# Where the split halves of the expert table lie, and when two small transposes are queued, in the second half of a streaming encoder layer

## The chip, the cores and the metric

The kernel runs on one core of a Trainium2 chip. A core has five engines with instruction queues of their own: PE (TensorE, matrix multiplies), DVE (VectorE), ACT (ScalarE), POOL (GpSimd) and SP (SyncE, which here only starts transfers). Each engine works through its queue in order, and semaphores tie the queues together. The metric is the device time of one launch in microseconds (us), the median of several runs.

## The reference, cut to what matters

One layer of an encoder for 384 tokens: 128 tokens of eight short sequences (the "sample" tokens) and 256 tokens of one prompt. After a recurrent branch and a sparse-attention branch comes PEER, a mixture of 16384 tiny experts, and only that part is touched here:

```python
q = (hb @ w_pq).reshape(PEER_BLOCK, PEER_HEADS, 2, PEER_DHALF)
s = jnp.einsum('nhpd,hpkd->nhpk', q, peer_keys).astype(jnp.float32)
s1, i1 = lax.top_k(s[:, :, 0], PEER_TOPK)
s2, i2 = lax.top_k(s[:, :, 1], PEER_TOPK)
...
sc, j = lax.top_k(cand, PEER_TOPK)
e = jnp.take_along_axis(cidx, j, axis=-1)
g = jax.nn.softmax(sc, axis=-1)
act = jax.nn.gelu(jnp.einsum('nhkd,nd->nhk', peer_u[e], hb).astype(jnp.float32))
return jnp.einsum('nhk,nhkd->nd', (g * act).astype(hb.dtype), peer_v[e])
```

Each token takes 8 x 16 = 128 of the 16384 experts. Expert e has a row of 1024 numbers in `peer_u` and one in `peer_v`.

## The kernel before

**Two ways through the experts.** For the 128 sample tokens the kernel gathers: 128 indirect transfers on POOL's queue (L1568, "picks"), each of 128 rows of 2048 numbers, into a ring of three buffers `raw`; DVE takes a product with a running sum (L1575), ACT the gelu (L1576, L1577), DVE adds the weighted row to `acc` (L1581). For the 256 prompt tokens it computes all 16384 experts densely, in 128 tiles of 128 experts: `dense_u(j)` loads tile j of the transposed `peer_u` (512 KB, into one of four buffers `w`) and multiplies it with the tokens `h2f`; gelu (L1484) puts the result in `G`. Later `weights` builds the matrix of picked weights out of one-hot products and multiplies it into G, and `dense_v` multiplies with `peer_v`.

**Two kinds of u tile.** Tiles 0 to 35 (N1 = 36) are multiplied as plain fp32, 8 matmuls of the program that appear as 16 in the profile. Tiles 36 and up are split first: ACT writes the high part `wh` (L230), DVE the low part `wl` (L234), and PE does 24 faster matmuls with the split tokens `h2h`, `h2l`. The split parts lie in a pool of their own, `halves2`, four buffers for wh and three for wl, 4 KB per partition each (28 KB).

**Selection.** `peer_select(i)` finds the 128 picks of each token of token tile i (i = 0: sample; 1 and 2: prompt): scores on PE, then some hundred small DVE instructions. For i = 1 and 2 it ends in three PE transposes of the result (indices `idx`, named pix in the profile, and weights `gw`, named pg; L1379) and one ACT copy into `pT` (L1381), which `weights` reads much later.

**Memory.** A partition's memory is handed out as two stacks, one growing from each end. At the left stand const, stream (the w buffers), and from L1656 on peer (raw, acc, h2h, h2l) and the pool of G. At the right stand hpool2, then qpool (h2f 8 KB, keysT 4 KB, qp 12 KB, ioe 0.5 KB), then sel (the selection's scratch, with idx and gw, about 31 KB). By the addresses that this kernel is given, 6,048 bytes are left between the end of G and the lower end of sel. So halves2 (L1679) is opened after `qs.close()` has closed qpool and sel, at the right end, where both lay. `late` (gA, gO) and the pool `wb` of `weights` follow below it.

**Order.** The program is written in the order of L1647 to L1724, and a scheduler then makes each engine's queue out of it: by a timing model of its own it runs the program and takes, for an engine that is free, the earliest instruction of the text that is ready. So picks, which the text spreads over the u tiles, stand far ahead, between the instructions of the selection. What is fixed at that point stays fixed: on the chip each queue runs in order. In `dense_v`'s loop a pick also waits for the matmuls of the fifth tile before (`pace`).

Of the kernel before, what the change touches and what calls it, by code (L numbers as in the profile page):

```python
# [182 lines left out]
OFF = [j for j in range(NW, 128) if (j - NW + 1) * NB // (128 - NW) > (j - NW) * NB // (128 - NW)]  # L183
AHEAD = sorted(OFF + [j for j in range(NW, 128) if j not in OFF][:NA - 1])
LAST, EARLY = 126, 108
WB, EB = (4, 4, 3), 3
UENG, VENG, GENG, VN = 'v', 'v', 'g', 3
SENG = 'gv'
# [7 lines left out]
class K:  # L196
# [1094 lines left out]
    def peer_select(self, i, h0=0, nh=8):  # L1291

        nc = self.nc
# [4 lines left out]
        for hb in range(0, nh, 4):  # L1298
            for half in range(2):
                pr = slice(64 * half, 64 * half + 64)  # L1300
                p = self.ps([128, 4, 128], tag="dx")
# [44 lines left out]
        idx = self.t([128, 2, 8, 16], tag="pix", bufs=2)[:, :, :nh]  # L1346
# [15 lines left out]
        gw = self.t([128, nh, 16], tag=f"pg{i}{h0}", pool=self.pool if i else self.hpool2)  # L1362
# [6 lines left out]
        gw = gw.rearrange("p a b -> p (a b)")  # L1369
        if i == 0:  # L1370
# [3 lines left out]
            nc.vector.tensor_copy(e, ef.rearrange("p h k -> p (h k)"))  # L1374
            return e, gw

        p = self.ps([128, 3, 128], tag="dx")
        for q, src in enumerate((idx[:, 0].rearrange("p h k -> p (h k)"), idx[:, 1].rearrange("p h k -> p (h k)"), gw)):
            nc.tensor.transpose(p[:, q], src, self.ident)  # L1379
        T = self.t([128, 3, 128], tag=f"pT{i}", pool=self.hpool2)  # L1380
# [85 lines left out]
    def dense_u(self, j):  # L1466

        nc = self.nc
        u = self.expert(self.I["puT"][j].rearrange("p k e -> p (k e)"))
        p = self.ps([128, 256], tag="u")  # L1470
        if j < N1:
            u = u.rearrange("p (k e) -> p k e", k=8)
            for k in range(8):
                self.mm(p, u[:, k], self.h2f[:, k], start=(k == 0), stop=(k == 7))
        else:
            uh, ul = (x.rearrange("p (k e) -> p k e", k=8) for x in self.split(u, UENG[j % len(UENG)]))
            hi, lo = self.h2p
            for k in range(8):
                self.mm(p, uh[:, k], hi[:, k], start=(k == 0), stop=False)
                self.mm(p, uh[:, k], lo[:, k], start=False, stop=False)  # L1480
                self.mm(p, ul[:, k], hi[:, k], start=False, stop=(k == 7))
        off = j in OFF
        g = self.G[:, j] if j < NW else self.t([128, 256], tag="gO" if off else "gA", bufs=2 if off else NA, pool=self.late)
        nc.scalar.activation(g, p, AF.Gelu_apprx_tanh)  # L1484
        if off:
            nc.sync.dma_start(self.Ad[OFF.index(j)], g)
        return g
# [97 lines left out]
    def run(self):  # L1585
        hs = self.ctx.enter_context(ExitStack())
        self.halves = self.open(hs, "halves")
        with ExitStack() as front:
            fh = front.enter_context(ExitStack())
            self.fconst = self.open(fh, "fconst")  # L1590
            self.hpool = self.open(fh, "hpool")
            self.fill = self.open(fh, "fill")
            self.psum = self.open(self.ctx, "psum", space=bass.MemoryType.PSUM)
            self.lo_pattern = "v"
            with ExitStack() as s:
                self.pool = self.open(s, "ph")
                self.setup()
                self.mod_head()
                self.front_x()
                self.front_h()  # L1600

                self.early = {name: self.raw(self.win_ap(name)) for name in ("wa", "wb", "wg")}
                with self.tc.issue_after(self.wdma.ins):
                    self.load_consts("cfront", self.fconst)
                    self.setup_front()
            self.lo_pattern = "v"
            self.gd = self.dt_([16, 128, NT])
            self.oad, self.obd = self.dt_([128, 8, NT]), self.dt_([128, 8, NT])
            with ExitStack() as s:
                rw = self.open(s, "rw")  # L1610
                self.pool = rw
                self.rwkv_head()
                self.rw = rw
                ds, n = None, dict.fromkeys("RGD", 0) | {"M": 8}
                for x in ORDER:
                    if x == "I":
                        with ExitStack() as s2:
                            self.pool = self.open(s2, "idx", side="right")
                            self.index()
                        ds = self.open(s, "dsa", side="right")  # L1620
                        continue
                    if x in "123":
                        self.pick_s() if x == "1" else self.pick_p("23".index(x))
                        continue
                    self.pool = rw if x == "R" else ds
                    self.lo_pattern = "g" if x == "g" else "v"
                    x = x.upper()
                    {"R": self.rwkv_pair, "M": self.mod_unit, "G": self.gate_unit, "D": self.dsa_quarter}[x](n[x])
                    n[x] += 1
                self.nc.sync.dma_start(self.O["sh"], self.last)  # L1630
            fh.close()
            self.hpool2 = self.open(self.ctx, "hpool2", side="right")
            qs = self.ctx.enter_context(ExitStack())
            self.qpool = self.open(qs, "qpool", side="right")
            with ExitStack() as s:
                mixp = self.pool = self.open(s, "mixp")
                self.mix()
                self.scores_head()
                for u in range(4):
                    self.out_unit(u)  # L1640
                sel = self.sel = self.open(qs, "sel", side="right")
                for i in range(3):
                    self.h2_tile(i)
        self.pool = sel
# [9 lines left out]
        T = [None] + [self.peer_select(i) for i in (1, 2)]  # L1654
# [9 lines left out]
        def pull(rate):  # L1664
            sn[0] += rate
            while sn[0] >= 1:
                sn[0] -= 1
                next(sparse, None)
# [7 lines left out]
        self.h2p = [self.t([128, 8, 256], F32R, tag=f"h2{x}", pool=self.peer) for x in "hl"]  # L1676
        self.hilo(*self.h2p, self.h2f, eng="v")
        qs.close()
        self.halves = self.open(self.ctx, "halves2", side="right")  # L1679
        self.late = self.open(self.ctx, "late", side="right")  # L1680
        for j in range(N1, NW):
            self.dense_u(j)
            pull(SR[0])

        def ahead(n):
            un[0] += UR
            if todo and un[0] >= 1 and todo[0] in AHEAD:
                un[0] -= 1
                u = todo.pop(0)
                gs[u] = self.dense_u(u)  # L1690
            pull(SR[1])

        with ExitStack() as s:
# [3 lines left out]
            nc = self.nc  # L1697
# [52 lines left out]
```

## Time and profile before

| what | us |
|---|---|
| median of 3 runs (1772.17 to 1779.79) | 1776.21 |
| the profiled execution, its own time | 1770.59 |
| span of its profile (granted PE clock 0.983) | 1768.8 |
| PE busy | 1672.8 (95%) |
| DVE busy | 1360.3 (77%) |
| ACT busy | 749.7 (42%) |
| POOL busy | 553.4 (31%) |

The profiled execution took 1.8 us more than its span, which is what lies around the first and the last instruction. Its stages, as far as this case needs them: the plain u tiles end at 1023.5 us of the span, the split tiles 36 to 75 at 1152, the weights and the tiles computed ahead at 1300, and the rest is the v stage. Matmuls overlap, so "busy" says little of PE; the number of matmuls that started in a stretch (the x behind the busy time) says more.

### The profile page before, as it was taken

The numbers are of one execution on the slowest core, as the hardware profiler recorded it, in microseconds if no ns is written. First come the engines' busy times: TensorE is split into PE (matmuls) and PEld (weight loads), VectorE is DVE, ScalarE is ACT, GpSimd is POOL, SyncE is SP. The second block draws the span as 40 slices with busy tenths as digits, with TensorE's granted clock in tenths as the row PEclk, the third lists the DMA queues.
The fourth block names the chain that finished last, engine by engine and source line by source line (L and its number), as shares of the span: only waits on it lengthen the run. The fifth ranks groups of instructions, "written<-read, shape, count | busy, mean of one in ns | idle before, by whom it ended". The sixth has DMA issues, their size and how long they took to land.

```text
span 1768.8 us, 33168 instructions
## 1 busy us (share of the span) xinstructions
PE 1672.8 (95%) x12424; PEld 1402.2 (79%) x12424; DVE 1360.3 (77%) x2902; ACT 749.7 (42%) x1652; POOL 553.4 (31%) x616
## 2 busy tenths in 40 slices
PE   6999899999999999998989889999989999999998
PEld 4988688778888877998878789999966667667766
DVE  3448878778867765555999999899867777877787
ACT  4433343334243333334233265577853333443344
POOL 1433343333342320024032223242243333333332
PEclk8999899999999999999999989999999999999999
DMA  8543662555364365755388989987559999999995
GB/s 301 161 123 103 185 194 67 153 175 153 94 215 140 105 204 191 235 189 185 125 333 323 342 302 389 374 330 263 192 203 393 342 367 363 374 356 390 344 382 215
DMA packets 172537, 436.71 MB, mean 247 GB/s; under 512 B 46036, under 2 KB 86100, under 8 KB 155992
## 3 DMA queue, kind: packets, MB, share of 16 engines
q1 hardware_dynamic: 153944, 300.36, 50.5%
q0 software_dynamic: 18432, 134.23, 19.9%
q8 instruction: 98, 1.61, 0.4%
q14 instruction: 63, 0.52, 0.1%
HBM read 403.23 MB, written 31.30 MB: 246 GB/s over the span
## 4 chain that ended last, share of the span: by engine, by line
PE 55%; DVE 19%; DMA 14%; issue 6%; ACT 3%; POOL 2%; SPq 1%; DVEq 0%; POOLq 0%; ACTq 0%
PE mm L226 20%; PE fx L226 13%; PE dx L226 9%; PE cp L226 6%; PE bx L226 5%; DMA w<-in_pv 3%; DMA raw<-in_puv,pe 3%; DVE wl L234 3%; DVE acc L1581 2%; DVE raw L1575 2%; DMA w<-in_puT 2%; ACT wh L230 1%; DMA w<-in_w_ada 1%; DMA w<-in_w_in 1%; DMA NL<-d 1%
## 5 line engine op out<-in xcount | busy, mean ns | idle before, releaser
L234 DVE TENSOR_TENSOR wl<-w,wh 128x1024 fp32r<-128x1024 f32 (+1 forms) x280 | 351.7, 1263 | 108.4 <-ACT wh L230 72.4
L230 ACT ACTIVATE wh<-w 128x1024 fp32r<-128x1024 f32 (+1 forms) x288 | 300.8, 1051 | 171.6 <-PE mm L226 77.2
L1568 POOL DMA_INDIRECT raw<-in_puv,pe x128 | 171.2, 1338 | 446.6 <-PE dx L226 156.5
L226 PE MATMUL fx<-h2h,wl 128*128 128x256 f32 x736 | 209.6, 285 | 8.8 <-DVE wl L234 8.8
L226 PE MATMUL fx<-h2h,wh 128*128 128x256 f32 x736 | 210.3, 286 | 3.0 <-ACT wh L230 2.8
L226 PE MATMUL fx<-h2l,wh 128*128 128x256 f32 x736 | 207.3, 282 | 0.0
L1581 DVE SCALAR_TENSOR_TENSOR acc<-raw,dots,acc 128x1024 f32<-128x1024 f32 x127 | 165.6, 1304 | 16.0 <-ACT dots L1577 15.7
L1575 DVE SCALAR_TENSOR_TENSOR raw<-raw,sh 128x1024 f32<-128x1024 f32 x128 | 160.3, 1252 | 7.7 <-DMA raw<-in_puv,pe 7.5
L226 PEld LDWEIGHTS fx<-h2h,wl 128*128 128x128 f32 x736 | 139.9, 190 | 12.5 <-DVE wl L234 12.1
L226 PEld LDWEIGHTS fx<-h2h,wh 128*128 128x128 f32 x736 | 139.9, 190 | 7.8 <-ACT wh L230 6.3
L226 PEld LDWEIGHTS fx<-h2l,wh 128*128 128x128 f32 x736 | 139.9, 190 | 1.7 <-issue 1.3
L226 PE MATMUL fx<-h2f,w 128*128 128x256 f32 x576 | 128.2, 382 | 11.5 <-ACT G L1484 11.5
L226 PEld LDWEIGHTS fx<-h2f,w 128*128 128x128 f32 x576 | 108.1, 190 | 29.7 <-ACT G L1484 14.9
L226 PE MATMUL mm<-LTh,wh 128*128 128x384 f32 (+2 forms) x352 | 123.2, 351 | 1.9 <-ACT wh L230 1.3
L226 PE MATMUL mm<-LTl,wh 128*128 128x384 f32 (+2 forms) x352 | 122.7, 349 | 0.5 <-POOL LTl L488 0.5
L226 PE MATMUL mm<-LTh,wl 128*128 128x384 f32 (+2 forms) x352 | 122.1, 347 | 0.0
L226 PE MATMUL mm<-wh,LTh 128*128 128x256 f32 x336 | 99.2, 296 | 2.9 <-ACT qx L888 2.9
L226 PE MATMUL mm<-wl,LTh 128*128 128x256 f32 x336 | 98.5, 293 | 0.0
L226 PE MATMUL mm<-wh,LTl 128*128 128x256 f32 x336 | 97.7, 291 | 0.0
L1576 ACT ACTIVATE dots<-dots 128x1 f32<-128x1 f32 x128 | 25.5, 199 | 161.7 <-DVE raw L1575 159.3
L226 PEld LDWEIGHTS mm<-LTh,wh 128*128 128x128 f32 (+2 forms) x352 | 66.2, 188 | 7.7 <-issue 3.0
L226 PEld LDWEIGHTS mm<-LTl,wh 128*128 128x128 f32 (+2 forms) x352 | 66.3, 188 | 3.2 <-issue 1.5
(571 smaller groups left out, 4152.3 us busy)
## 6 DMA issues: line engine op xcount, KB each, us to landing
w<-in_puT SPq DMA_DIRECT2D x128, 512.0 KB
w<-in_pv SPq DMA_DIRECT2D x128, 512.0 KB
w<-in_w_in SPq DMA_DIRECT2D x70, 512.0 KB
w<-in_w_ada SPq DMA_DIRECT2D x48, 512.0 KB
cKT<-in_cKT SPq DMA_DIRECT2D x32, 256.0 KB
cV<-in_cV SPq DMA_DIRECT2D x32, 256.0 KB
w<-in_w_pq SPq DMA_DIRECT2D x16, 512.0 KB
d<-wst SPq DMA_DIRECT2D x8, 832.0 KB
```

Of the source, the lines that this page charges most:

```text
L226: return self.nc.tensor.matmul(out, l, r, start=start, stop=stop, skip_group_check=True, **kw)
L230: self.nc.scalar.activation(hi, src, AF.Copy)
L234: (self.nc.vector if eng == "v" else self.nc.gpsimd).tensor_tensor(lo, src, hi, op=OP.subtract)
L1568: d = nc.gpsimd.indirect_dma_start(out=bass.AP(tensor=u.tensor, offset=u.offset, ap=[u.ap[0], [1, 2048]]), out_offset=None, in_=self.I["puv"],
L1575: nc.vector.scalar_tensor_tensor(u, u, 1.0, h2, op0=OP.mult, op1=OP.mult, accum_out=dot)
L1576: nc.scalar.activation(dot, dot, AF.Gelu_apprx_tanh)
L1581: nc.vector.scalar_tensor_tensor(acc, v, dot, acc, op0=OP.mult, op1=OP.add)
```

## The change

Four things. Pool sel is opened ahead of qpool, so that qpool is the inner one of the two and can be closed while sel stays open. halves2 is opened at the left end, above G. sel stays open through the split tiles 36 to 75, and late is opened after it is closed. And the transposes with their copy leave `peer_select` for a method `turn`, called after tile 37 (for i = 1) and tile 44 (for i = 2), with its PE instructions kept behind the last matmul of that tile.

```diff
 LAST, EARLY = 126, 108
+TP = (37, 44)
...
             return e, gw
 
+        return idx, gw
+
+    def turn(self, i, idx, gw):
+
+        nc = self.nc
         p = self.ps([128, 3, 128], tag="dx")
         for q, src in enumerate((idx[:, 0].rearrange("p h k -> p (h k)"), idx[:, 1].rearrange("p h k -> p (h k)"), gw)):
             nc.tensor.transpose(p[:, q], src, self.ident)
...
-                self.mm(p, ul[:, k], hi[:, k], start=False, stop=(k == 7))
+                self.ulast = self.mm(p, ul[:, k], hi[:, k], start=False, stop=(k == 7))
...
             self.hpool2 = self.open(self.ctx, "hpool2", side="right")
+            ss = self.ctx.enter_context(ExitStack())
+            sel = self.sel = self.open(ss, "sel", side="right")
             qs = self.ctx.enter_context(ExitStack())
             self.qpool = self.open(qs, "qpool", side="right")
...
-                sel = self.sel = self.open(qs, "sel", side="right")
...
         qs.close()
-        self.halves = self.open(self.ctx, "halves2", side="right")
-        self.late = self.open(self.ctx, "late", side="right")
+        self.halves = self.open(self.ctx, "halves2")
         for j in range(N1, NW):
             self.dense_u(j)
+            if j in TP:
+                with self.tc.issue_after(self.ulast.ins):
+                    i = 1 + TP.index(j)
+                    T[i] = self.turn(i, *T[i])
             pull(SR[0])
+        ss.close()
+        self.late = self.open(self.ctx, "late", side="right")
```

## The prediction, written before the changed kernel was run

> **What bounds the kernel now.** I read the stretches first, cut where the kinds of tile change (per engine: busy us, instructions begun; then granted clock, DMA share, GB/s).
>
> ```profile
> core 0: us, PE busy (x) PEld busy (x) DVE busy (x) ACT busy (x) POOL busy (x), PEclk, DMA share, GB/s
> ...
> 880.00:1023.50 143.50, 132.02 (x616) 112.14 (x615) 139.40 (x543) 43.55 (x111) 40.10 (x33) 1.00 0.89 325
> 1023.50:1029.70 6.20, 0.76 (x4) 0.33 (x3) 6.01 (x14) 2.41 (x6) 3.20 (x2) 0.69 0.86 288
> 1029.70:1036.00 6.30, 6.15 (x27) 5.86 (x28) 6.30 (x9) 3.25 (x5) 0.09 (x1) 0.50 0.97 345
> 1036.00:1152.00 116.00, 114.12 (x986) 113.31 (x986) 105.69 (x123) 67.26 (x146) 36.41 (x23) 1.00 0.94 362
> 1152.00:1300.00 148.00, 139.81 (x1200) 137.91 (x1200) 141.12 (x197) 118.27 (x311) 46.14 (x37) 1.00 0.69 243
> 1300.00:1769.00 469.00, 449.28 (x1910) 321.96 (x1910) 354.91 (x422) 183.71 (x371) 159.40 (x126) 0.99 0.92 347
> ```
>
> See two short rows in a dense table: for 6.2 us PE starts 4 matmuls, and for the next 6.3 us it has half its clock. From 1036 to 1300 PE is nearly full, with DVE close behind (141.1 of 148 in the last part), and the v stage is held by PE and DMA together. The row that gives PE's full pace is the fullest of the 20 us stretches, with its neighbours, which I need for the DMA rate too:
>
> ```profile
> 1080.00:1100.00 20.00, 20.00 (x179) 20.00 (x178) 17.15 (x19) 10.20 (x21) 6.43 (x5) 1.00 1.00 397
> 1100.00:1120.00 20.00, 19.24 (x169) 19.04 (x168) 15.75 (x18) 10.68 (x22) 4.67 (x4) 1.00 0.98 369
> 1120.00:1140.00 20.00, 19.15 (x165) 18.75 (x164) 18.66 (x21) 9.77 (x20) 8.05 (x5) 1.00 0.97 372
> 1140.00:1160.00 20.00, 19.73 (x170) 19.53 (x169) 18.42 (x22) 13.99 (x33) 11.25 (x8) 1.00 0.94 373
> ```
>
> 179 in 20 us is 0.112 us per split matmul, 2.7 us per tile of 24. Next, the timeline of PE, DVE and ACT around the hole, start and length in us, in brackets the wait before:
>
> ```profile
> 1019.91 3.62 PE L226 MATMUL fx<-h2f,w 128*128 128x256 f32 x16
> ...
> 1026.34 1.05 DVE L1360 TENSOR_REDUCE pix<-poh 128x64 f32<-128x256 bf16 x2
> ...
> 1027.45 0.48 PE L1379 MATMUL dx<-cfirst,pix 128*128 128x128 f32 x1 [3.92 <-DVE pix L1360]
> ...
> 1028.17 0.49 ACT L1381 ACTIVATE pT<-dx 128x384 f32<-128x384 f32 x1 [1.60 <-PE dx L1379]
> ...
> 1028.56 2.94 ACT L230 ACTIVATE wh<-w 128x1024 fp32r<-128x1024 f32 x3
> ...
> 1029.66 0.58 PE L226 MATMUL fx<-h2h,wh 128*128 128x256 f32 x1 [1.52 <-ACT wh L230]
> ```
>
> The last plain tile ends at 1023.5. PE then stands at the transposes of i = 2, in order, until DVE has written the last pix. After them the first three wh are copied back to back: the tiles lay loaded and waited for the place of sel, whose last readers these transposes are. So the selection's end holds the first split tile twice, in PE's queue and by memory.
>
> **The change part by part.** *What the hole costs PE.* 6.20 us less 4 matmuls of 0.112 is 5.75; 6.30 us less 27 of 0.112 is 3.28. Together 9.0 us. The clock fell after a wait of 3.9 and 1.5 us with little between; a shorter wait left it alone (this row lies in a stretch of clock 1.00):
>
> ```profile
> 995.35 3.72 PE L226 MATMUL fx<-h2f,w 128*128 128x256 f32 x16 [1.93 <-ACT G L1484]
> ```
>
> The Trainium skill ("TensorE: Matmul & The Clock Gate", "What's actually happening") says that an idle window of about 3.4 us halves the clock and about 3.4 us of sustained work restores it. The fall agrees; the way back does not: the trace shows some 6 us of matmuls at 0.50. By the page the half clock would cost about 1.7 us and the hole 7.5 instead of 9.0; the measured row decides.
>
> *What takes its place.* What DVE and ACT do from 1036 to 1152, in groups (busy us, mean ns of one, the wait before):
>
> ```profile
> L234 DVE TENSOR_TENSOR wl<-w,wh 128x1024 fp32r<-128x1024 f32 x38 | 46.3, 1223 | 7.9 <-ACT wh L230 7.4 <-issue 0.3 <-PE fx L226 0.2
> L230 ACT ACTIVATE wh<-w 128x1024 fp32r<-128x1024 f32 x38 | 39.8, 1054 | 6.8 <-DMA w<-in_puT 5.3 <-PE fx L226 1.4
> ...
> L1581 DVE SCALAR_TENSOR_TENSOR acc<-raw,dots,acc 128x1024 f32<-128x1024 f32 x22 | 28.2, 1281 | 1.5 <-ACT dots L1577 1.5
> L1575 DVE SCALAR_TENSOR_TENSOR raw<-raw,sh 128x1024 f32<-128x1024 f32 x22 | 26.9, 1221 | 0.9 <-DMA raw<-in_puv,pe 0.8
> ...
> L1396 DVE TENSOR_TENSOR oh<-wA,wB 128x512 f32<-128x512 f32 x9 | 5.9, 688 | 0.0
> ...
> L1443 DVE TENSOR_TENSOR oh<-pT,dx 128x512 f32<-128x512 f32 x4 | 2.7, 682 | 0.0
> ```
>
> Whose memory must the new halves wait for?
>
> ```profile
> L226 PEld LDWEIGHTS dx<-keysT,qp x96: 182/188/188, 840.2 to 962.0; 64*128 64x128 f32 x96
> L226 PE MATMUL fx<-h2f,w x576: 379/379/483, 879.7 to 1023.2; 128*128 128x256 f32 x192
> ```
>
> qpool now begins 6,048 bytes above G, with h2f lowest (8 KB), then keysT (4), qp (12), ioe. From G's end up lie wh 0 (in the free bytes), wh 1 to 3 (over h2f, the last also over keysT), then the three wl (over keysT and qp). So wh 0 and all wl are free from about 962, and wh 1 to 3 when the last plain tile is done at 1023.5. Tile 36 can be split before PE needs it. Tile 37 needs a copy of 1.05 us and a subtraction of 1.22 (the mean of one in L230 and L234) after 1023.5, by about 1025.9 if DVE is free, while PE is in tile 36 until 1026.2: nothing is lost. If instead the whole pool must be free, or wl 36 stands behind other work, PE waits for wh (1.05), wl (1.22) and one product of DVE (1.3, L1581): 3.6 us, which lies between the 1.9 that left the clock alone and the 3.9 with 1.5 that did not; with the clock lost it would be 3.6 + 3.3 = 6.9. Between 0 and 6.9 I take 0.5, as each address speaks for it. Late next is DVE: it is full here (6.01 of 6.20 busy), so a wl goes in only where the scheduler put it.
>
> *What is moved.* Six transposes and two copies of 0.49 us; none issues a DMA. Behind tile 37 and 44, at about 1029 and 1023.5 + 9 x 2.7 = 1048, they stand in PE's queue ahead of the next tile, and in ACT's the copy ahead of later wh. Their inputs were there by 957.5 (i = 1, this row) and 1027.4 (i = 2),
>
> ```profile
> 957.50 0.27 PE L1379 MATMUL dx<-cfirst,pg 128*128 128x128 f32 x1
> ```
>
> so they cost their own 0.112 each, as before. Up to nine wl (9 x 1.22 = 11.0 us) may now go ahead of the selection's tail and bring it to 1038.4, still 10 us short of 1048. Cost 0; if that cover is gone, the hole is back.
>
> *What comes later.* Pools late and wb lie in sel's place, so `weights` cannot prepare batches before 1048 (now: from 1028.6). The one-hots begin as soon as pT is there, and the batches' results wait for the last gelu into G (count, ns, first and last start):
>
> ```profile
> L1443 DVE TENSOR_TENSOR oh<-pT,dx x32: 671/677/685, 1028.6 to 1296.6; 128x512 f32<-128x512 f32 x32
> L1484 ACT ACTIVATE G<-fx x76: 361/384/389, 889.7 to 1151.4; 128x256 f32<-128x256 f32 x76
> L1408 DVE TENSOR_TENSOR G<-G,mm x32: 455/460/472, 1151.8 to 1298.6; 128x304 f32<-128x304 f32 x32
> ```
>
> Until 1152 there are 5.9 + 2.7 = 8.6 us of one-hots, moved from the crowded start to the rest of a stretch in which DVE has 116.00 - 105.69 = 10.3 us free: cost 0, its cover being these 10.3 us.
>
> *What of the 9.0 - 0.5 = 8.5 us arrives.* From 1023.5 to 1152 the DMAs brought 288 x 6.2 + 345 x 6.3 + 362 x 116 = 45.95 MB. At the mean of the four fullest rows, 378 GB/s, that takes 121.6 us instead of 128.5: 6.9 us less. At 362 it takes 126.9: 1.6 less. If picks (1 MB each) slide into the next stretch, whose DMA share is 0.69, all 8.5 pass, but a pick brings DVE 1.28 + 1.22 = 2.5 us there. Between 1.6 and 8.5 I take 6.0, near the 6.9, since the four fullest rows show that rate held for 80 us. The rest of the way hands it on: all picks that may run ahead of the v stage are gone well before its start. POOL busy on picks, and their number, by stretch:
>
> ```profile
> 880.00:1023.00 143.00, 34.57 (x27) 1.00 0.89 325
> 1023.00:1031.00 8.00, 3.29 (x2) 0.68 0.93 307
> 1031.00:1152.00 121.00, 36.32 (x22) 0.98 0.94 361
> 1152.00:1300.00 148.00, 11.55 (x7) 1.00 0.69 243
> 1300.00:1320.00 20.00, 1.79 (x1) 1.00 0.64 219
> ```
>
> 27 + 2 + 22 + 7 = 58, then one in 20 us and the rest paced by v tiles. The text pulls 55 before the v stage and 3 for its five unpaced tiles, also 58. So 1152 to 1300 and the v stage have the same work, begun earlier.
>
> **Sum.** 1770.6 - 6.0 = 1764.6 for the profiled execution; on the median of the three runs, which is 5.6 above that execution, 1776.2 - 6.0 = 1770.
>
> **The rivals.** *The hole moves or the DMAs eat it.* PE's next tile waits for wl behind the selection (3.6), or at tile 44, and DMA gives 1.6 only: between 0 and -2.5, 1775. For it: DVE is busy for 139.4 of the 143.5 us of the plain tiles. Against: DMA has 0.86 in the hole.
> *More than the hole.* All 8.5 pass, and with the one-hots gone from the start PE's waits from 1036 to 1152 (116 - 986 x 0.112 = 5.6) shrink by 4: -12.5, 1764. For it: wl stood in line with one-hots; against: ACT waited 5.3 there for tiles still on the way.
> *Slower.* The one-hots miss the room before 1152, as sel is freed too late, and land in 1152 to 1300, where DVE has 148 - 141.1 = 6.9 us free over all: they cost up to 8.6 us, with digits, factors and their ACT halves some 11. With 6.0 gained, +5: 1781. It decides if the batches' first matmuls come after about 1140. For it: memory delays them by 20 us. Against: 100 us remain.
> *By the page's rule on the clock*, any wait over about 3.4 us at tile 44 would halve the clock again; with the 3.28 measured here, a wait of 6 there would make 9 and leave the time at 1776. I put it into the first rival.
>
> **How the numbers follow.** Forecast 0.47, hole moved 0.23, more 0.20, slower 0.10. About 0.5% (8.9 us) is what a measurement of this kernel can tell from no change. Beyond it on the fast side (under 1767.3): "more" 0.20 and 0.08 of the forecast's spread, 0.28. Beyond it on the slow side needs the late one-hots with no gain, 1787: 0.07. Within: 0.65. Range: from "more" 1764 less the 4 us by which the three runs scatter, and 1 for a longer one, 1759; up to the slower case and 1, 1782.
>
> **What would show it.** Right: the first matmul with h2h follows the last with h2f within 1 us, near 1023.5; clock 1.00 throughout 1020 to 1040; pT of i = 2 near 1048; the last gelu into G near 1145 instead of 1151.4; 58 picks before the v stage; DMA above 362 GB/s until then. Wrong: PE waits of over 2 us for wl or at L1379; the first one-hot after 1100; or the same early start with the last G at 1150, the time lost to w still on its way. The forecast fails as a whole if the scheduler, given other places, orders the v stage otherwise; no row here can bound that, and the range holds some 5 us of it.

## The result, and the profile after

| | before | after |
|---|---|---|
| median of 6 runs each, us | 1775.66 (1772.17 to 1779.79) | 1788.96 (1785.32 to 1792.90) |
| ratio of the two, with its 95% interval | | 1.0065 [1.0046, 1.0085] |
| the profiled execution, its own time | 1770.59 | 1789.28 |
| span of its profile | 1768.8 | 1787.5 |

The change makes the kernel slower, by 13.3 us between the medians and 11.5 by the ratio, outside the range of the prediction and on the side that had 0.07. The lines of the changed file lie one further down up to the selection's end and six behind it: the matmuls are now L227, wh is L231, wl L235, the picks L1574 to L1587, the turn L1385 and L1387. The ratio here and those below are the recorded ones, each against runs of the kernel before from the same session (medians 1775.03 to 1776.51 in the later ones), so they are not the quotients of the medians shown.

First the table of stretches of the changed kernel, cut like the one of before: plain tiles, hole, first split tiles, the other split tiles, weights, v stage.

```profile
core 0: us, PE busy (x) PEld busy (x) DVE busy (x) ACT busy (x) POOL busy (x), PEclk, DMA share, GB/s
886.80:1028.80 142.00, 132.34 (x612) 112.64 (x612) 137.43 (x543) 43.12 (x107) 35.29 (x32) 0.99 0.87 316
1028.80:1033.60 4.80, 0.39 (x2) 0.00 (x0) 4.20 (x8) 1.74 (x5) 0.95 (x1) 0.98 0.97 331
1033.60:1040.20 6.60, 6.11 (x27) 5.82 (x28) 6.21 (x8) 2.58 (x5) 2.85 (x2) 0.50 1.01 400
...
1100.00:1120.00 20.00, 20.00 (x169) 20.00 (x169) 18.41 (x22) 10.17 (x21) 6.72 (x4) 1.00 0.99 376
1120.00:1140.00 20.00, 20.00 (x169) 20.00 (x168) 16.21 (x17) 8.64 (x19) 4.58 (x4) 1.00 0.99 388
...
1161.30:1316.70 155.40, 147.04 (x1211) 144.82 (x1210) 143.92 (x202) 119.99 (x318) 45.79 (x40) 0.98 0.68 240
1316.70:1787.50 470.80, 453.30 (x1904) 323.52 (x1902) 361.62 (x422) 182.77 (x368) 147.28 (x126) 1.00 0.93 346
```

Two things are to be seen. The hole is still there: 4.8 us in which PE starts 2 matmuls, and again 6.6 us at half the clock with 27 of them. And in the two rows where PE has no gap at all, 20.00 of 20 busy, it starts 169 matmuls. The fullest row of before had 179. PE is as busy as it was and does less.

Next the timelines of PE around 1088 us, where both kernels run split tiles one behind the other at clock 1.00; first before, then after.

```profile
1087.84 0.28 PE L226 MATMUL fx<-h2h,wh 128*128 128x256 f32 x1
...
1088.86 0.28 PE L226 MATMUL fx<-h2h,wh 128*128 128x256 f32 x1
```

```profile
1087.90 0.28 PE L227 MATMUL fx<-h2h,wh 128*128 128x256 f32 x1
...
1088.86 0.28 PE L227 MATMUL fx<-h2h,wl 128*128 128x256 f32 x1
```

Before, 9 steps take 1.02 us, 113 ns each; after, 8 steps take 0.96, 120 ns. The length in the second column, 0.28, is the same in both and tells nothing, since the matmuls overlap: only the starts show the pace. The tiles of before at 1088 us have the faster of two paces that occur there (more under "The form alone"). In the u tiles that run without a wait the mean step is 115.4 before and 120.0 after; in the v stage (128x512) the usual step is 227 and 233.5 (the means, with the steps between groups, are 228.0 and 233.4). No operand, shape or count of these matmuls differs, only where the tiles lie.

From the first matmul of the prompt's queries on (845.5 and 852.5 us; up to there both programs run in the same order, and the 7 us are scatter between executions) the profiled executions of all kernels divide as follows. I use this part for comparisons, as it leaves the scatter of the front out; each row is still one execution.

| us | queries to last plain matmul | to last gelu into G | to the end | sum |
|---|---|---|---|---|
| before | 177.7 | 128.2 | 617.4 | 923.3 |
| after | 176.3 | 132.5 | 626.2 | 935.0 |
| pad64 | 173.5 | 130.5 | 619.6 | 923.6 |
| pad32 | 175.7 | 129.6 | 626.2 | 931.5 |
| pad96 | 176.1 | 129.0 | 626.6 | 931.6 |
| p192 | 176.2 | 129.0 | 623.0 | 928.2 |
| before_pad64 | 178.1 | 130.2 | 617.8 | 926.1 |
| vplace | 176.3 | 130.8 | 623.4 | 930.5 |
| whfirst | 174.0 | 127.5 | 621.1 | 922.6 |
| first2 | 175.9 | 130.9 | 620.1 | 926.9 |
| noturn | 177.2 | 125.0 | 619.0 | 921.2 |
| turn38 | 174.2 | 131.6 | 619.5 | 925.3 |
| short5 | 177.5 | 128.5 | 618.0 | 924.0 |

After is 11.7 us behind before: +4.3 in the stretch in which the gain was to come, +8.8 behind it.

### The profile page after: what moved, and what is told of

Same layout as the page of the kernel before. It is cut to its first block, busy times and chain, and to the rows that moved or that the text cites. A ratio compares the mean times of both kernels' runs of the same rounds, so it can differ in the third digit from the quotient of the medians.

```text
span 1787.5 us, 33161 instructions
## 1 busy us (share of the span) xinstructions
PE 1693.2 (95%) x12424; PEld 1418.7 (79%) x12424; DVE 1365.5 (76%) x2902; ACT 748.2 (42%) x1652; POOL 536.7 (30%) x616
## 3 DMA queue, kind: packets, MB, share of 16 engines
q0 software_dynamic: 18432, 134.23, 19.9%
## 4 chain that ended last, share of the span: by engine, by line
PE 55%; DVE 20%; DMA 10%; issue 8%; ACT 3%; POOL 2%; SPq 0%; DVEq 0%; POOLq 0%; ACTq 0%
PE mm L227 19%; PE fx L227 13%; PE dx L227 10%; PE cp L227 6%; PE bx L227 6%; DVE wl L235 3%; DMA raw<-in_puv,pe 3%; DVE raw L1581 2%; DMA w<-in_pv 2%; DVE acc L1587 2%; ACT wh L231 1%; DMA w<-in_w_in 1%; DVE TX L699 1%; DMA NL<-d 1%; DMA w<-in_w_ada 1%
## 5 line engine op out<-in xcount | busy, mean ns | idle before, releaser
L235 DVE TENSOR_TENSOR wl<-w,wh 128x1024 fp32r<-128x1024 f32 (+1 forms) x280 | 354.6, 1274 | 96.8 <-ACT wh L231 56.3
L231 ACT ACTIVATE wh<-w 128x1024 fp32r<-128x1024 f32 (+1 forms) x288 | 300.3, 1050 | 156.1 <-PE mm L227 79.6
L1574 POOL DMA_INDIRECT raw<-in_puv,pe x128 | 168.0, 1313 | 450.2 <-PE dx L227 169.7
L227 PE MATMUL fx<-h2h,wh 128*128 128x256 f32 x736 | 215.2, 292 | 7.4 <-ACT wh L231 7.2
L227 PE MATMUL fx<-h2h,wl 128*128 128x256 f32 x736 | 213.8, 291 | 6.2 <-DVE wl L235 5.9
L227 PE MATMUL fx<-h2l,wh 128*128 128x256 f32 x736 | 211.4, 287 | 0.0
L1587 DVE SCALAR_TENSOR_TENSOR acc<-raw,dots,acc 128x1024 f32<-128x1024 f32 x127 | 168.6, 1328 | 19.0 <-ACT dots L1583 18.7
L1581 DVE SCALAR_TENSOR_TENSOR raw<-raw,sh 128x1024 f32<-128x1024 f32 x128 | 159.2, 1244 | 12.0 <-DMA raw<-in_puv,pe 11.7
L227 PEld LDWEIGHTS fx<-h2h,wh 128*128 128x128 f32 x736 | 143.7, 195 | 12.7 <-ACT wh L231 10.3
L227 PEld LDWEIGHTS fx<-h2h,wl 128*128 128x128 f32 x736 | 143.3, 195 | 9.7 <-DVE wl L235 8.9
L227 PEld LDWEIGHTS fx<-h2l,wh 128*128 128x128 f32 x736 | 143.8, 195 | 1.8 <-issue 1.1
L227 PE MATMUL fx<-h2f,w 128*128 128x256 f32 x576 | 129.1, 385 | 9.3 <-ACT G L1490 9.2
L227 PEld LDWEIGHTS fx<-h2f,w 128*128 128x128 f32 x576 | 109.4, 192 | 28.0 <-ACT G L1490 12.9
L227 PE MATMUL mm<-LTh,wh 128*128 128x384 f32 (+2 forms) x352 | 124.1, 353 | 1.6 <-ACT wh L231 1.0
L227 PE MATMUL mm<-LTl,wh 128*128 128x384 f32 (+2 forms) x352 | 123.4, 351 | 1.0 <-POOL LTl L489 1.0
L227 PE MATMUL mm<-LTh,wl 128*128 128x384 f32 (+2 forms) x352 | 122.8, 349 | 0.0
L227 PE MATMUL mm<-wh,LTh 128*128 128x256 f32 x336 | 99.9, 298 | 2.9 <-ACT qx L889 2.9
L227 PE MATMUL mm<-wl,LTh 128*128 128x256 f32 x336 | 99.1, 295 | 0.0
L227 PE MATMUL mm<-wh,LTl 128*128 128x256 f32 x336 | 98.3, 293 | 0.0
L227 PEld LDWEIGHTS mm<-LTh,wh 128*128 128x128 f32 (+2 forms) x352 | 66.8, 190 | 7.5 <-issue 3.0
L227 PEld LDWEIGHTS mm<-LTl,wh 128*128 128x128 f32 (+2 forms) x352 | 66.8, 190 | 3.7 <-issue 1.5
```

Source lines behind the costliest of these rows:

```text
L227: return self.nc.tensor.matmul(out, l, r, start=start, stop=stop, skip_group_check=True, **kw)
L231: self.nc.scalar.activation(hi, src, AF.Copy)
L235: (self.nc.vector if eng == "v" else self.nc.gpsimd).tensor_tensor(lo, src, hi, op=OP.subtract)
L1574: d = nc.gpsimd.indirect_dma_start(out=bass.AP(tensor=u.tensor, offset=u.offset, ap=[u.ap[0], [1, 2048]]), out_offset=None, in_=self.I["puv"],
L1581: nc.vector.scalar_tensor_tensor(u, u, 1.0, h2, op0=OP.mult, op1=OP.mult, accum_out=dot)
L1587: nc.vector.scalar_tensor_tensor(acc, v, dot, acc, op0=OP.mult, op1=OP.add)
```

## The experiments

Three theories on the pace: (A) it depends on where the two operands of a matmul start, counted modulo some power of two; (B) parts at the far end of memory are faster; (C) something else in the new order of the queues. By the addresses that the programs are given, h2h and h2l start at 160 modulo 256 in every kernel of the layer. wh and wl start at 224 before and at 160 after; Gh and Gl at 224 in both.

### The place of the parts: pad64, pad32, pad96, before_pad64, p192

```diff
         self.halves = self.open(self.ctx, "halves2")
+        self.t([128, 16], tag="pad", pool=self.halves)
```

That is pad64: 16 numbers, 64 bytes per partition. pad32 has 8 of them, pad96 24, p192 48. before_pad64 is the kernel before with the right end 64 bytes lower:

```diff
+            pad = self.open(self.ctx, "pad", side="right")
+            self.t([128, 16], tag="pad", pool=pad)
             self.hpool2 = self.open(self.ctx, "hpool2", side="right")
```

> The changed kernel with 64 unused bytes ahead of the split halves, so that every wh and wl lies 64 bytes higher (in the kernel before they lay at 96 past a multiple of 128 bytes, in the changed one at 32, here at 96 again); same program order. Theory A, the start of the halves within 128 bytes sets the pace of the split matmuls: starts of these matmuls 113 to 118 ns apart instead of 120, and about 16 us less, 1773. Theory B, what counts is the far end of the memory they lay in before: 120 ns and 1789 as the changed kernel. Theory C, the pace has nothing to do with the place and the time was lost in the order of the queues: 1789 too, with the 120 ns left unexplained.

> The changed kernel with 32 unused bytes ahead of the halves, which then start at a multiple of 64 that is not one of 128. Theory A does not say which of the four places in 128 bytes are fast: anything from 109 to 120 ns; if a start at a multiple of 64 is what counts, this one and the next are the fastest of all, below 113 ns, 1765 to 1773. Theories B and C: 120 ns, 1789.

> The changed kernel with 96 unused bytes ahead of the halves, which then start at a multiple of 128. Theory A: a pace other than 120 ns, the same as with 32 bytes if 64 bytes are the unit. Theories B and C: 120 ns, 1789.

> The kernel before with 64 unused bytes at the far end of its memory, so that all that grows from that end, the halves among it, lies 64 bytes lower: halves at 32 past a multiple of 128, where the changed kernel has them, but still at the far end. Theory A: 120 ns and about 16 us more than before, 1792. Theory B and C: 113 to 118 ns as before and 1776.

> The changed kernel with 192 bytes (per partition) ahead of the halves instead of 64. If the unit of the place is 128 bytes (wh again at 96 of 128, h2h at 32): split u tiles at 113 to 118 ns start to start, v at 227 ns as with 64, and a time as with 64, 1777 within 4. If what counted with 64 bytes was another distance (a larger unit, 256 or more): another pace, up to 120 and 234 ns, and up to 1789.

The distance is that of the stationary operand's start from the moving one's, modulo 256. In a u tile wh is stationary and h2h moves; in the v stage Gh is stationary and wh moves.

| kernel | u: distance, mean ns per step | v: distance, usual ns per step | median us | ratio to before |
|---|---|---|---|---|
| before | 64, 115.4 | 0, 227 | 1775.66 | 1 |
| after | 0, 120.0 | 64, 233.5 | 1788.96 | 1.0065 [1.0046, 1.0085] |
| pad64 | 64, 115.6 | 0, 227 | 1777.71 | 1.0009 [0.9985, 1.0033] |
| pad32 | 32, 118.3 | 32, 233 | 1785.89 | 1.0051 [1.0033, 1.0070] |
| pad96 | 96, 117.9 | 224, 234 | 1783.89 | 1.0050 [1.0026, 1.0075] |
| p192 | 192, 117.6 | 128, 232.7 | 1782.16 | 1.0026 [1.0005, 1.0047] |
| before_pad64 | 0, 120.0 | 0, 227 | 1781.26 | 1.0028 [1.0010, 1.0047] |

Sixty-four bytes bring the loss back to nothing that can be measured, and the same sixty-four bytes bring the kernel before to 120 ns and make it slower by 0.28%. The pads leave the order of every compute queue as it was. So (A) holds for the pace, (B) and (C) fall. The times lie closer together than I expected (pad64 1773, before_pad64 1792): I had put the whole effect at 16 us. My first unit was wrong too: p192 has the same place as pad64 within 128 bytes and not its pace (232.7 in the v stage).

### The form alone: pace

A program that computes nothing of the layer: two moving and two stationary tensors, tiles of 24 matmuls in the order of a u tile and groups of 12 in the order of the v stage, at 16 distances.

```python
for d in range(0, 512, 32):
    u(f"u{d}", d // 4, 0, 4)      # 4 tiles of 24, stationary part d bytes further on
```

> The split matmuls by themselves: none of the layer is computed and the outputs are zeros. Tiles of 24 matmuls of 128x256 (two moving tensors, two stationary, the order of a u tile) with the start of the stationary part moved in steps of 32 bytes from 0 to 480 bytes behind that of the moving part, then the same two distances (0 and 64) with both moved, then products of 128x512 in the order of the v stage, again with 16 distances; no other engine works. If the place alone sets the pace: 128x256 at 120 ns at 0, 118 at 32, 113 to 118 at 64, 118 at 96, 117.5 at 192, and 128x512 at 227 at 0 and 232 to 234 at 32, 64, 128 and 224; moving both changes nothing; perhaps a distance that neither kernel has is faster still. If it is a contest with the other engines for the memory: the same pace at every distance, within 1 ns.

Mean step in ns, from the starts in the trace (96 matmuls of 256 columns and 48 of 512 for each distance):

| distance | 0 | 32 | 64 | 96 | 128 | 160 | 192 | 224 | 256 | 288 | 320 |
|---|---|---|---|---|---|---|---|---|---|---|---|
| 128x256 | 120.0 | 118.3 | 117.8 | 117.4 | 120.0 | 120.0 | 117.8 | 117.9 | 119.9 | 118.3 | 117.8 |
| 128x512 | 230.2 | 233.1 | 233.4 | 234.1 | 232.5 | 233.4 | 229.1 | 233.2 | 226.8 | 233.1 | 233.4 |

From 256 on the numbers repeat (352 to 480 do too), but for the first v group, which follows another form. Moving both parts by 32, 64, 128 or 256 bytes leaves 119.9 to 120.0 at distance 0 and 117.8 at 64. No other engine works here, so the differences are not a contest with other engines for memory: in this program the pace goes by the distance modulo 256, and the v numbers agree with those of the layer within 1 ns.

The distance is not the whole rule. At distance 64 the layer has tiles at 113.3 and tiles at 117.8, the form alone has 117.8 only. It is not the buffer: in the kernel before, the tile at 1068.1 us runs at 117.8 and that at 1101.8 at 113.3, with wh and wl in the same places. The pace comes in trains: in before, 311 steps in a row from 1072.3 us on are at 113 and 117 in a row from 1137.6 on at 118, and the longest trains begin right behind a wait or a one-hot product. In the changed kernel, at distance 0, the tiles without a wait all have 119.6 to 120.0. What chooses between the two paces at 64 stays open.

The Trainium skill ("TensorE: Matmul & The Clock Gate", "Wait — 56ns, not 53.3ns?") gives the step of warm back-to-back matmuls as columns over 2.4 GHz and about 2.5 ns, 215.7 for 512 columns, with no word on where the operands lie. For 256 columns that makes 109.2, an estimate from the section's formula. No mean step here reaches either figure (the nearest are 113.3 and 226.8), and the part above it, 4 to 18 ns, changes with the distance; the measurement decides.

### The v stage's part: vplace

The changed kernel with only the parts of G, and what lies below them at the right end, moved by 64 bytes: u distance 0, v distance 0.

```diff
+        pad = self.open(self.ctx, "pad", side="right")
+        self.t([128, 16], tag="pad", pool=pad)
         self.pool = self.open(self.ctx, "dv", side="right")
```

> The changed kernel with only the parts of G (and what lies below them at the right end) 64 bytes lower, so that in the v stage the stationary and the moving part start at the same place of 256 bytes, and the u tiles stay at the slow place. If the place sets the pace of each form by its own pair: 128x512 at 227 ns instead of 233.5, 128x256 still at 120, and of the loss of some 12 us the v stage's part gone, 1104 x 6.4 ns = 7 us: 1782, the time of the kernel before with its u tiles at the slow place. If the v stage is held by its DMAs: the pace changes, the time stays at 1787 to 1789.

The timelines of PE in the v stage, one row and the same row of the next tile, 12 matmuls later; first after, then vplace:

```profile
1502.14 0.39 PE L227 MATMUL bx<-wl,Gh 128*128 128x512 f32 x1
...
1504.94 0.39 PE L227 MATMUL bx<-wl,Gh 128*128 128x512 f32 x1
```

```profile
1499.34 0.39 PE L227 MATMUL bx<-wl,Gh 128*128 128x512 f32 x1
...
1502.06 0.39 PE L227 MATMUL bx<-wl,Gh 128*128 128x512 f32 x1
```

2.80 us against 2.72, 233 against 227 ns: the pace came back as expected. The time came back by less: 1785.19, ratio 1.0051 [1.0030, 1.0072], where 1782 was expected. Its interval overlaps that of the changed kernel, so the runs don't show clearly that any time came back. In the profiles it is 4.5 us of the 11.7, but 1.7 of them lie ahead of the last gelu into G, where no v matmul runs, and are scatter. The DMA share of the changed kernel is 0.93 in the v stage, so I take it that PE waits part of its gain away there; that is argued, not shown.

### The hole: whfirst and first2

The timeline of ACT and that of DVE in the changed kernel, between the last plain matmul (1028.8) and the first split one (1033.6):

```profile
1031.82 0.20 ACT L1582 ACTIVATE dots<-dots 128x1 f32<-128x1 f32 x1 [4.19 <-DVE raw L1581]
1032.06 0.29 ACT L1583 ACTIVATE dots<-dots,pg 128x1 f32<-128x1 f32 x1
1032.26 0.36 ACT L1490 ACTIVATE G<-fx 128x256 f32<-128x256 f32 x1
1032.52 1.99 ACT L231 ACTIVATE wh<-w 128x1024 fp32r<-128x1024 f32 x2
```

```profile
1029.59 1.06 DVE L1361 TENSOR_REDUCE pix<-poh 128x64 f32<-128x256 bf16 x2
1030.56 1.22 DVE L1581 SCALAR_TENSOR_TENSOR raw<-raw,sh 128x1024 f32<-128x1024 f32 x1
```

The first wh stands in ACT's queue behind the gelu of a pick; that pick's product stands in DVE's queue behind the last pix of the selection. So the selection's end still holds the first split tile, by another way. whfirst (64 bytes of pad, as all kernels from here on but short5) keeps every pick's gelu from no. 24 on behind the first wh:

```diff
-                nc.scalar.activation(dot, dot, AF.Gelu_apprx_tanh)
+                d = nc.scalar.activation(dot, dot, AF.Gelu_apprx_tanh)
+                if q * PH * 16 + j >= PICK:
+                    self.tc.add_manual_dep(d.ins, self.wh0.ins.name, ...)
```

> The changed kernel with 64 bytes ahead of the halves, and ACT's gelu of every pick from no. 24 on kept behind the first wh copy in ACT's queue. If the hole now comes from ACT's order (wh of tile 36 behind the gelu of a pick, that behind the selection's tail on DVE): from the last matmul with h2f to the first with h2h 2.5 us or less instead of 4.9, clock 1.00 after it, and the 40 tiles 4 to 6 us earlier; the time 1772 to 1776 if the DMAs let it through, 1777 if they take it back later. If it comes from memory or the arrival of w: the hole stays at 4 us or more, 1777. If DVE loses more by picks held back than PE gains: 1780 or more.

The first gap shrank to 1.8 us, and the wait went to DVE's queue. whfirst's stretches right behind:

```profile
1022.90:1025.60 2.70, 0.50 (x2) 0.30 (x2) 2.45 (x4) 1.12 (x3) 0.00 (x0) 0.95 0.98 364
1025.60:1028.60 3.00, 2.99 (x14) 2.99 (x15) 0.91 (x1) 0.33 (x1) 0.00 (x0) 0.50 1.01 421
```

Two matmuls, then a wait for wl, then half the clock for 3 us. The time is 1779.06, ratio 1.0024 [1.0005, 1.0044]: no gain. first2 therefore puts both parts of the first two tiles first: besides the ACT order, the DVE product of pick 24 stands behind wl of tile 36, that of the later picks behind wl of tile 37, and the gelu of tile 35 behind wh of tile 36 (its lines lie up to 15 further down than those of the changed kernel: the matmuls are L229, wh is L233, the gelu of a u tile L1500).

```diff
+                n = q * PH * 16 + j
+                if n >= PICK:
+                    hi, lo = self.halfs[min(n - PICK, 1)]
+                    self.behind(m, lo)
+                    self.behind(d, hi)
...
+            if j == N1:
+                self.behind(self.nc.scalar.activation(self.G[:, N1 - 1], self.last_p, AF.Gelu_apprx_tanh), self.halfs[0][0])
```

> The changed kernel with 64 bytes ahead of the halves, and the first two split tiles put first in the queues: the gelu of tile 35 behind the first wh on ACT, and the picks from no. 24 (25) on behind wl and wh of tile 36 (37) on DVE and ACT. If the hole was the order of the two queues alone: PE waits under 2 us in all from the last plain matmul to the end of tile 37, clock 1.00, from there to the last gelu into G 122 to 123 us (130.5 with the 64 bytes alone, 128.2 before), and 1769 to 1772, faster than both. If the loads of tile 37 or the selection still stand ahead: waits of 3 us or more and 1775 to 1778. If the gain is given back in the weights or the v stage: those waits gone, but 1775 or more.

Its table of stretches from the last plain matmul on, the wh copies out of ACT's timeline, and a wait of PE's:

```profile
1022.00:1036.00 14.00, 10.19 (x79) 9.18 (x78) 11.43 (x17) 7.93 (x15) 2.62 (x2) 1.00 0.93 353
...
1038.00:1041.40 3.40, 3.40 (x18) 3.40 (x17) 3.40 (x4) 0.10 (x1) 1.68 (x1) 0.51 0.98 384
```

```profile
1022.45 1.06 ACT L233 ACTIVATE wh<-w 128x1024 fp32r<-128x1024 f32 x1 [1.70 <-PE fx L229]
...
1024.11 1.06 ACT L233 ACTIVATE wh<-w 128x1024 fp32r<-128x1024 f32 x1 [0.33 <-DMA w<-in_puT]
...
1027.07 1.06 ACT L233 ACTIVATE wh<-w 128x1024 fp32r<-128x1024 f32 x1 [0.43 <-DMA w<-in_puT]
...
1032.40 1.06 ACT L233 ACTIVATE wh<-w 128x1024 fp32r<-128x1024 f32 x1 [0.85 <-DMA w<-in_puT]
```

```profile
1036.42 0.39 PE L229 MATMUL fx<-h2h,wh 128*128 128x256 f32 x1 [1.77 <-ACT G L1500]
```

In the first 14 us the clock stays at 1.00 and PE starts 79 matmuls. Tiles 36 and 37 are through 8.4 us behind the last plain matmul, in pad64 13.9; PE waits 2.1 us for their parts, about what was expected. But from tile 37 on each wh now starts when its w lands. At 1036.4 PE has waited 1.8 us for a gelu, and then it has half the clock for 3.4 us. The 105th split matmul comes 19.9 us behind the last plain one, in pad64 20.8: most of the lead is gone within 20 us, and the stretch to the last gelu into G takes 130.9 us, no less than pad64's 130.5. The time is 1779.57, ratio 1.0023 [1.0007, 1.0040].

### What a gain at this place is worth: short5

The kernel before, without the two low-part products of tiles 38 to 42 (75 matmuls); all loads, splits, gelus and picks stay.

```diff
-                self.mm(p, uh[:, k], lo[:, k], start=False, stop=False)
-                self.mm(p, ul[:, k], hi[:, k], start=False, stop=(k == 7))
+                if j not in SHORT: self.mm(p, uh[:, k], lo[:, k], start=False, stop=False)
+                if j not in SHORT or k == 7: self.mm(p, ul[:, k], hi[:, k], start=False, stop=(k == 7))
```

> The kernel before without the two low-part products of tiles 38 to 42 (15 of 24 matmuls each, 75 in all); every load, split, gelu and pick stays. PE has 75 x 0.1154 = 8.7 us less to do right behind the hole, about what closing the hole would have given. If what PE gains there arrives: from the last plain matmul to the last gelu into G 119.5 us instead of 128.2, and 1767 to 1768. By the step that took 6.0 of 8.5: 1770. If DMAs or DVE take it back before the v stage or in it: 1774 or more.

The stretch from the last plain matmul to the last gelu into G, before and then short5 (with three of its parts ahead), and ACT's group of wh copies in the same stretch, before and then short5:

```profile
1023.20:1151.40 128.20, 121.00 (x1014) 119.35 (x1012) 117.70 (x143) 72.32 (x154) 39.55 (x24) 0.96 0.94 357
```

```profile
1040.60:1060.00 19.40, 18.13 (x125) 16.89 (x126) 19.40 (x28) 15.35 (x37) 4.63 (x3) 0.87 0.81 298
1060.00:1080.00 20.00, 16.26 (x122) 15.86 (x123) 20.00 (x26) 11.34 (x26) 6.32 (x4) 0.91 0.86 329
1080.00:1100.00 20.00, 19.42 (x165) 19.02 (x164) 16.35 (x18) 9.64 (x20) 4.68 (x4) 1.00 1.00 385
...
1034.30:1162.80 128.50, 116.37 (x939) 113.01 (x937) 117.32 (x143) 72.01 (x154) 39.76 (x24) 0.96 0.93 358
```

```profile
L230 ACT ACTIVATE wh<-w 128x1024 fp32r<-128x1024 f32 x41 | 42.8, 1053 | 6.8 <-DMA w<-in_puT 5.3 <-PE fx L226 1.4
```

```profile
L230 ACT ACTIVATE wh<-w 128x1024 fp32r<-128x1024 f32 x41 | 42.9, 1053 | 16.1 <-DMA w<-in_puT 12.5 <-PE fx L226 3.5
```

PE starts 75 matmuls fewer, 8.7 us of its work at 115.4 ns, in 0.3 us more. DVE and ACT do the same number of instructions, the DMAs bring the same (357 x 128.2 = 45.8 MB, 358 x 128.5 = 46.0 MB), and what PE gains is lost again, most of it in waits: the wh copies stand 12.5 us for w instead of 5.3. Part goes to the clock, which is halved once more for 3.4 us at 1066.1, in the row with 0.91; that is 1.7 us, half of the 3.4. The time is 1780.29, ratio 1.0016 [0.9993, 1.0038], where 1767 to 1770 would have meant that the gain arrives. So in this stretch PE is full but does not set its length. The rows say what may: up to 1080 us DVE has no gap (19.40 of 19.40 and 20.00 of 20) while the DMAs stand at 0.81 and 0.86, and from there on the DMAs are full (1.00). The rows of before in the prediction show the same: DVE 6.01 of 6.20 and 6.30 of 6.30, later DMA shares from 0.94 to 1.00. So it looks like DVE first and the DMAs after; no run here takes work from either alone, so these two are not parted by experiment.

### The transposes and the late release: noturn and turn38

noturn puts the transposes back at the end of each selection, turn38 calls `turn` for i = 2 after tile 38.

```diff
-        return idx, gw
+        return self.turn(i, idx, gw)
...
-            if j in TP:
-                with self.tc.issue_after(self.ulast.ins):
-                    i = 1 + TP.index(j)
-                    T[i] = self.turn(i, *T[i])
```

```diff
-TP = (37, 44)
+TP = (37, 38)
```

> The changed kernel with 64 bytes ahead of the halves, and the transposes back at the end of each selection, ahead of the split tiles. If the moved transposes took a stall out of PE's queue: the hole grows from 4.9 us to 6 or more, and the time to 1779 to 1781. If another wait (wh of tile 36 behind the selection's tail in ACT's queue) ends last anyway: hole within 1 us of 4.9 and time within 2 of 1777.7.

> The changed kernel with 64 bytes ahead of the halves, and the transposes of i = 2 behind tile 38 instead of 44. If the late release of the selection's memory costs the weights' stage its 3.7 us (stretch from the last gelu into G to the first v tile): the first one-hot matmul at about 1055 instead of 1071, that stretch 3 to 4 us shorter, 1774. If the late release costs nothing: first one-hot matmul as early, but the same time, 1777 within 2. If the one-hots crowd DVE at the start of the tiles: up to 3 slower.

noturn came out in neither way: its first gap is 1.8 us, since the scheduler now put the first wh ahead of the selection's tail; two matmuls later PE stands 2.0 us at the transposes of i = 2, until the last pix is there. 1777.04, ratio 1.0006 [0.9982, 1.0031], like pad64: so the transposes' place and the new order of ACT's queue together are worth nothing that can be measured; this run does not part the two. The moved transposes are not free where they stand, though. In the changed kernel PE's longest wait in the split tiles behind 1040 us comes right after those of i = 2 (1063.5):

```profile
1063.84 0.49 ACT L1387 ACTIVATE pT<-dx 128x384 f32<-128x384 f32 x1
1064.23 0.28 ACT L1583 ACTIVATE dots<-dots,pg 128x1 f32<-128x1 f32 x1
1064.41 2.00 ACT L231 ACTIVATE wh<-w 128x1024 fp32r<-128x1024 f32 x2
```

```profile
1065.51 0.39 PE L227 MATMUL fx<-h2h,wh 128*128 128x256 f32 x1 [1.47 <-ACT wh L231]
```

ACT's copy into pT waits for the transposes, and a wh copy stands behind it. In turn38 this wait is gone, but another of 2.5 us appears, up to 1102.5; the first one-hot matmul comes at 1057.6 instead of 1070.8 in pad64, and the stretch from the last gelu into G to the first v tile is 1.4 us shorter, not 3 to 4. The time is 1781.34, ratio 1.0012 [0.9985, 1.0040]: the late release costs nothing that shows. None of the twelve kernels beats the kernel before.

## Why the prediction was wrong, step by step

- **A term was missing.** The sum priced only queues and waits, and the cost of the move of halves2 itself was nothing. Moving it set the distance in the u tiles from 64 to 0 and in the v stage from 0 to 64. By the steps that is 2208 x 4.6 ns = 10.2 us for the u tiles and 1104 x 6.5 = 7.2 for the v stage; with the means of the v stage, 228.0 and 233.4, it is 6.0. Of these 16 to 17 us about 10 to 11 arrive (ratio 1.0065 against 1.0009 with pad64, 935.0 against 923.6 in the profiles). This is all of the loss that can be measured, and it is why the sign was wrong. "The v stage has the same work" was true and not enough.
- **"What takes its place", 0.5 us with bounds 0 to 6.9.** It was wrong by memory and by the queues. By memory wh 36 was to be free from about 962 and split before PE needs it. In first2, where nothing stands ahead of it in ACT's queue, it still starts only when the last plain matmul is done (its row above, 1022.45, released by PE), although by the addresses that the program is given its bytes lie below h2f. The other end, "the whole pool must be free", fits that. PE then waits 1.15 us for wh and 0.93 for wl, 2.1 us instead of 0.5. By the queues, I had named "wl 36 stands behind other work", and that came about on ACT as well. The gap of 4.8 less two steps of 0.12, and 6.6 us at half clock less 27 of 0.12, make 7.9 us in the changed kernel: above the upper bound, 1.1 below the hole of before rather than 8.5. The clock was misread on the way: the row of the hole of before has a mean of 0.69, and 6.2 us at that mean are 3.8 us at half, so the clock fell some 2.4 us into the first wait and not after 3.9 and 1.5. A wait of 1.9 is not safe either: in first2 one of 1.8 was followed by half the clock.
- **"What of the 8.5 us arrives", 6.0 with bounds 1.6 to 8.5.** This step would have failed even with the hole closed. short5 gave PE 8.7 us at this place and the stretch grew by 0.3: nothing arrives, and even the lower bound was too high. The step priced the DMAs alone, at 378 GB/s from the four fullest rows and at 362 from the stretch behind the hole; over the whole stretch it is 357 and in short5 358. It did not count DVE right behind the hole, which in short5 is busy without a gap from 1034 to 1080 us. The first rival (the DMAs eat it, 1775) is the nearest, with the DMAs as the only cause. With the place mended its time also comes out: pad64, 1777.71, ratio 1.0009 [0.9985, 1.0033].
- **"What is moved", cost 0.** Off by about 1.5 us at tile 44, in ACT's queue as described there. The transposes of i = 2 came 34.5 us behind the last plain matmul, not 24.5, by the hole and the slower pace. That this reaches the end is not seen: noturn, without them there, has a ratio of 1.0006, pad64 1.0009.
- **"What comes later", cost 0.** Right in kind: the first one-hot matmul comes 27 us later, counted from the last plain matmul, and the slower rival did not come about. In pad64 the time from the last gelu into G to the last one-hot matmul is 152.8 us, before 152.6. The time ended beyond that rival's 1781 for a reason that it does not contain.
- **58 picks before the v stage:** right, in both kernels.

## What to carry to other kernels

Two programs with the same matmuls need not run them at the same pace: when a change moves a matmul operand in memory, compare the start-to-start step of each form before anything else, and keep (or choose) the distance of the two operands' starts modulo 256 bytes on purpose. An engine that is full is not always the one that sets a stretch: leave some of its work out at the place of a hoped-for gain, and see whether the stretch gets shorter. Memory that comes free earlier helps only if the instruction that waits for it does not stand, in its engine's queue, behind what used to hold the memory.

## What the hardware showed that I had not expected

- The step of matmuls of the same shape, at full clock and without other work on the core, goes from 117.4 to 120.0 ns (256 columns) and from 226.8 to 234.1 (512) with the distance of the two operands modulo 256 bytes; in the layer also 113.3. The best distances differ: 64 for the u form among the five that the layer's kernels have, where 0 is the worst, and 0 for the v form. What in the chip makes this is not shown.
- A wait of 1.4 us, two matmuls and one of 2.2 us were enough to halve the clock in whfirst, where it came back after some 3 us of matmuls; in first2 one wait of 1.8 us was followed by 3.4 us at half. After the holes of 6.2 and 4.8 us it took 6.3 and 6.6.
